# Four small half-row products behind the spreading of the token scale, in six places of a four-layer decoder trunk

## The chip, the cores and the metric

The kernel runs on one core of one Trainium2 chip. The metric is device time in microseconds (us) for one execution. Several executions are timed, and the figure for a kernel is the median of them. One more execution is recorded instruction by instruction; its own time stands beside the median below.

## The reference

The trunk has four layers on 256 tokens of width 1024. Each layer has a token mixer (layers 0 and 3: dilated window attention; layer 1: short gated convolution; layer 2: a conformer convolution module), and then a gated convolutional channel mixer with an inner width of 2816. RMS normalisation stands before and after every sub-layer:

```python
def conv_ffn(x, w_in, w_conv, w_out):
    u = causal_dwconv(x @ w_in, w_conv)
    g, v = jnp.split(u, 2, axis=-1)
    return (jax.nn.silu(g) * v) @ w_out

    for i in range(DEPTH):
        a = rms_norm(h, mix_norm_pre[i])
        ...
        h = h + rms_norm(m, mix_norm_post[i])
        f = conv_ffn(rms_norm(h, ffn_norm_pre[i]), ffn_w_in[i], ffn_w_conv[i], ffn_w_out[i])
        h = h + rms_norm(f, ffn_norm_post[i])
```

All inputs are float32, and 253.87 MB of weights are read once.

## The kernel before, in words

Features lie on the 128 partitions and the 256 tokens on the free axis, so an activation of width 1024 is eight tiles of 128x256. A weight is split into two parts for accuracy: ScalarE copies the high part (`whi`, L192) and VectorE subtracts it from the original to get the low part (`wlo`, L198). Activations are split in the same way. Each product of a weight tile (128x128, the stationary operand) with an activation tile (128x256, the moving operand) is then three TensorE instructions: high by high, high by low, low by high. `mm3` issues them at L280, L281 and L282; `Slabs.mm` issues the same three at L522. A piece of 1024 weight columns is thus 24 products.

Every mixer begins with `start_norm` (L449): a "ramp" (L433, L438, L440) over the first four pieces with the activations not yet divided by their root mean square, and in it `rstd_of` (L306), which reduces the squares over the partitions. The scale per token, r, has to lie along the free axis in all partitions; `spread` (L320 to L324) makes it so with two products of r, broadcast, with the identity (each is two passes in the trace, so four rows of L324). `spread_later` (L333) defers this: it gives back a function that calls `spread` and copies the result out of PSUM on ScalarE (L336). The channel mixer (`ffn`), `short_conv` and `conformer` hand that function to the next `column` (L462), which calls it behind the first 9 of its 24 products. Attention calls `spread` in another way and does not use `spread_later`.

A channel mixer has 22 pairs of columns; the ramp has done two pairs, and the other 20 pairs follow (L280 to L282, into PSUM banks of the pools A and B), with products of finished inner channels with the output weights between them and behind them (14 "slabs" and 8 pieces of "tail", L522). These are 62 pieces of 24 products, of which the first 9 products lie ahead of the spread. In all of them the stationary operand is a weight.

In attention two kinds of products differ. `scores` (L897) takes the product of queries and keys of two heads at a time, and a head is 64 rows: the two heads' products lie on rows 0 to 63 and rows 64 to 127 and alternate, each into a bank of its own. `value` (L878, L879, L880) has the activation as the stationary operand and the weight as the moving one. `warm` (L331) issues products of no use while TensorE would wait.

The kernel is written in program order; a framework adds the semaphores. Each engine runs its instructions in that order.

Of the kernel before, what the change touches and what calls it, by code (L numbers as in the profile page):

```python
# [10 lines left out]
F32 = mybir.dt.float32  # L11
# [5 lines left out]
P = 128  # L17
# [7 lines left out]
DH = 64  # L25
# [203 lines left out]
def trunk_kernel(ctx: ExitStack, tc: tile.TileContext, xT, pos, params, consts, masks, w8, out):  # L229
    nc = tc.nc  # L230
# [30 lines left out]
    def act(dt=F32, tag="act", bufs=NACT, shape=(P, 2, T)):  # L261
        counter[0] += 1
        return ap.tile(list(shape), dt, tag=tag, name=f"{tag}{counter[0]}", bufs=bufs)

    def two():
        t = act(F32R)
        return t[:, 0, :], t[:, 1, :]
# [7 lines left out]
    def psum(tag="A"):  # L275
        counter[0] += 1
        return ps.tile([P, 512], F32, tag=tag, name=f"ps{tag}{counter[0]}", bufs={"A": 4, "B": 3, "S": 1}[tag])
# [6 lines left out]
    def TT(out, a, b, op):  # L284
        nc.vector.tensor_tensor(out=out, in0=a, in1=b, op=op)  # L285
# [14 lines left out]
    def rstd_of(accs):  # L300


        ms = psum("S")
        for i, acc in enumerate(accs):
            for c in range(2):
                nc.tensor.matmul(ms[:, c:c + 1], lhsT=acc[:, c * P:(c + 1) * P], rhs=ones[:, 0:1],  # L306
                                 start=i == 0 and c == 0, stop=i == len(accs) - 1, skip_group_check=True)
        v, y, u, r = tiny(), tiny(), tiny(), tiny()
        nc.vector.reciprocal(out=v, in_=ms[:, 0:2])
        nc.scalar.activation(out=y, in_=ms[:, 0:2], func=AF.Sqrt)  # L310
        TT(u, y, y, ALU.mult)
        TT(r, y, v, ALU.mult)
        STT(u, u, -0.5, v, ALU.mult, ALU.mult)
        STT(r, u, 1.5, r, ALU.add, ALU.mult)
        return r
# [4 lines left out]
    def spread(r):  # L320

        rb = psum("S")[:, :T]
        for c in range(2):
            nc.tensor.matmul(rb[:, c * P:(c + 1) * P], lhsT=r[:, c:c + 1].to_broadcast([P, P]), rhs=ident,  # L324
                             start=True, stop=True)
        return rb
# [3 lines left out]
        for _ in range(n):  # L330
            nc.tensor.matmul(o, lhsT=ident, rhs=cst[:, :T], start=True, stop=True)  # L331

    def spread_later(r):  # L333

        rb = act()[:, 0, :]
        return rb, lambda: nc.scalar.copy(out=rb, in_=spread(r))  # L336

    def bc2(a):
        return a.rearrange("p (s t) -> p s t", s=1).to_broadcast([P, 2, T])
# [85 lines left out]
    def ramp(xs, os, hook=None):  # L425


        ws = [st.take() for _ in os]
        alone = [i == 0 or os[i - 1].tensor is not o.tensor for i, o in enumerate(os)]

        def second(k):
            for o, (whi, wlo, _) in zip(os, ws):
                nc.tensor.matmul(o, lhsT=whi[:, k, :], rhs=xs[k][1], start=False, stop=k == KD - 1,  # L433
                                 skip_group_check=True)

        for k in range(KD):
            for o, (whi, wlo, _), a in zip(os, ws, alone):
                nc.tensor.matmul(o, lhsT=whi[:, k, :], rhs=xs[k][0], start=k == 0 and a, stop=False,  # L438
                                 skip_group_check=True)
                nc.tensor.matmul(o, lhsT=wlo[:, k, :], rhs=xs[k][0], start=False, stop=False,  # L440
                                 skip_group_check=True)
            if k:
                second(k - 1)
        if hook:
            hook()
        second(KD - 1)
        return os

    def start_norm(xs, acc, os):  # L449

        r = []
        ramp(xs, os, lambda: r.append(rstd_of([acc])))
        return r[0]
# [5 lines left out]
    def halves(t):  # L459
        return [t[:, e * T:(e + 1) * T] for e in range(2)]  # L460
# [96 lines left out]
    def ffn(l, mg, rb):  # L557
        xs, acc = boundary(mg, rb, f"fpre{l}")
        gs = []

        pend = []

        def gate(last=False):

            ts = pend.pop(0)
            TT(ts[1], ts[0], ts[1], ALU.mult)
            x = two()
            nc.scalar.copy(out=x[0], in_=ts[1])
            st.diff()
            TT(x[1], ts[1], x[0].bitcast(F32), ALU.subtract)  # L570
            st.copy()
            gs.append(x)

        def evac(bank, f):
            u = act()
            TT(u, bank[:].rearrange("p (s t) -> p s t", s=2), bc2(rb), ALU.mult)
            ts = taps3([u[:, e, :] for e in range(2)], f"fconv{l}_", (f, KF + f), between)
            nc.scalar.activation(out=ts[0], in_=ts[0], func=AF.Silu)
            pend.append(ts)
            if len(pend) > 1:  # L580
                gate()
            if f == KF - 1:
                gate()

        banks = [psum("A") for _ in range(4)] + [psum("B") for _ in range(3)]
        rb, scale = spread_later(start_norm(xs, acc, halves(banks[0]) + halves(banks[1])))
        nc.scalar.preload_act_table(AF.Silu)
        slabs, out_ = Slabs(), None
        for what, i in ffn_steps():
            if what == "col":  # L590
                if i > 1:
                    bank = banks[i] if i < 7 else psum("B")
                    for o in halves(bank):
                        column(xs, o, scale)
                        if scale:
                            for f in range(2):
                                evac(banks[f], f)
                        scale = None
                    evac(bank, i)
                    between()  # L600
            elif what == "slab":
                slabs.add(gs[i])
                between()
            else:
                if out_ is None:
                    out_ = Out(f"fpost{l}")
                o = slabs.tail(i, gs[FF_HEAD:])
                out_.evac(i, o)
                if out_.n < KD - 1:
                    st.pump(2)  # L610
        return out_.end()


    def short_conv(l, mg, rb):
        xs, acc = boundary(mg, rb, f"mpre{l}")
        banks = [psum(a) for a in "AAAABB"]
        os = halves(banks[0]) + [banks[1][:, :T], banks[2][:, :T]]
        rb, scale = spread_later(start_norm(xs, acc, os))
        rb2 = act()[:, 0, :]
        os.append(column(xs, banks[2][:, T:], scale))  # L620
        nc.scalar.activation(out=rb2, in_=rb, func=AF.Square)
        os.append(column(xs, banks[3][:, :T]))
        ys = []
        slabs, out_ = Slabs(), None
        for what, k in sc_steps():
            if what == "col":
                if k > 1:
                    o1, o2 = banks[4:6] if k == 2 else (psum("B"), psum("B"))
                    os = halves(o1) + [o2[:, :T]]
                    for o in os:  # L630
                        column(xs, o)
                c, hh, b = os[:3]
                os = os[3:]
                t, y = tmp(), tmp()
                nc.scalar.copy(out=t, in_=c)
                TT(t, hh, t, ALU.mult)
                TT(t, t, rb2, ALU.mult)
                u, = taps3([t], "sconv", [k], between)
                TT(y, b, rb, ALU.mult)
                TT(y, y, u, ALU.mult)  # L640
                x = two()
                nc.scalar.copy(out=x[0], in_=y)
                between()
                TT(x[1], y, x[0].bitcast(F32), ALU.subtract)
                between()
                ys.append(x)
            elif what == "slab":
                slabs.add(ys[k])
                between()
            else:  # L650
                if out_ is None:
                    out_ = Out(f"mpost{l}")
                o = slabs.tail(k, ys[SC_HEAD:])
                out_.evac(k, o)
                if out_.n < 4:
                    st.pump(1)
        return out_.end()


    def conformer(l, mg, rb):  # L660
        xs, acc = boundary(mg, rb, f"mpre{l}")
        NP = KD // 2
        banks = [[psum("A") for _ in range(2)] for _ in range(2)]
        rb, scale = spread_later(start_norm(xs, acc, halves(banks[0][0]) + halves(banks[0][1])))
        nc.scalar.preload_act_table(AF.Sigmoid)
        us, ts, os = [None] * NP, [None] * NP, [None] * NP

# [88 lines left out]
        r = rstd_of([s[:, e, :] for s in sq[2:] for e in range(2)] + [sq[0][:, 0, :]])  # L756
        warm(3)
        rb = spread(r)
# [3 lines left out]
        for q in range(NP):  # L762
            if q:
                TT(us[q], us[q], bc2(rb), ALU.mult)
            for e in range(2):
# [4 lines left out]
                x, y = two(), tmp()  # L770
# [13 lines left out]
        for d in range(4, KD):  # L784
            o = column(ys, psum("B")[:, :T])
# [310 lines left out]
    with tc.manual_schedule():  # L1096
# [15 lines left out]
        mg, rb = None, None  # L1112
        for l in range(DEPTH):
            mg, rb = (attention, short_conv, conformer)[l % 3](l, mg, rb)
# [3 lines left out]
            mg, rb = ffn(l, mg, rb)  # L1118
# [83 lines left out]
```

## Time and profile before

| what | value |
|---|---|
| median of 3 runs | 1577.72 us |
| the three runs | 1564.25, 1577.72, 1581.02 us |
| profiled execution, its own time | 1583.57 us |
| profiled execution, span | 1581.7 us |
| mean granted TensorE clock | 0.996 |
| TensorE busy | 98% of the span |
| VectorE, ScalarE busy | 79%, 58% |

The span runs from the first to the last instruction of the profiled execution. Matmuls overlap each other in TensorE, so their durations do not add up to time; what a stretch of them costs is read from the distance between the starts of successive ones. The granted clock is given as a share of full speed.

### The profile page before, as it was taken

The numbers are of one execution on the slowest core, as the hardware profiler recorded it, in microseconds if no ns is written. First come the engines' busy times: TensorE is split into PE (matmuls) and PEld (weight loads), VectorE is DVE, ScalarE is ACT, GpSimd is POOL, SyncE is SP. The second block draws the span as 40 slices with busy tenths as digits, with TensorE's granted clock in tenths as the row PEclk, the third lists the DMA queues.
The fourth block names the chain that finished last, engine by engine and source line by source line (L and its number), as shares of the span: only waits on it lengthen the run. The fifth ranks groups of instructions, "written<-read, shape, count | busy, mean of one in ns | idle before, by whom it ended". The sixth has DMA issues, their size and how long they took to land.

```text
span 1581.7 us, 31426 instructions
## 1 busy us (share of the span) xinstructions
PE 1555.7 (98%) x13146; PEld 1520.5 (96%) x13146; DVE 1243.0 (79%) x2177; ACT 925.2 (58%) x1623; POOL 17.9 (1%) x51
## 2 busy tenths in 40 slices
PE   6999999999999999999999999999999999999998
PEld 6999999999999999999999999999999999999997
DVE  4997877697876779889599598786887778588783
ACT  6564655575564566656477666565655445566562
POOL 4000000000000000000000000000000000000000
PEclk9999999999999999999999999999999999999999
DMA  5653543265552644655243136554453434236540
GB/s 218 216 212 131 176 145 108 99 232 204 187 190 100 217 161 162 238 187 184 110 144 124 54 118 239 197 174 153 178 192 138 161 134 160 107 134 237 190 160 28
DMA packets 36718, 256.94 MB, mean 162 GB/s; under 512 B 4320, under 2 KB 4448, under 8 KB 5984
## 3 DMA queue, kind: packets, MB, share of 16 engines
q1 hardware_dynamic: 36288, 254.93, 45.0%
q8 instruction: 103, 1.69, 0.4%
q14 instruction: 39, 0.32, 0.1%
q10 hardware_dynamic: 288, 0.01, 0.0%
HBM read 253.87 MB, written 1.05 MB: 161 GB/s over the span
## 4 chain that ended last, share of the span: by engine, by line
PE 93%; DVE 3%; ACT 1%; POOL 1%; issue 1%; DMA 1%; DVEq 0%; ACTq 0%; POOLq 0%
PE psA L522 17%; PE psB L282 10%; PE psB L280 10%; PE psB L281 10%; PE psA L280 7%; PE psA L281 7%; PE psA L282 7%; PE psA L878 3%; PE psA L880 3%; PE psA L879 3%; PE psB L715 2%; PE psB L926 2%; PE psB L897 2%; PE psA L438 2%; PE psB L915 2%; PE psA L433 2%
## 5 line engine op out<-in xcount | busy, mean ns | idle before, releaser
L198 DVE TENSOR_TENSOR wlo<-raw,whi 128x1024 fp32r<-128x1024 f32 x480 | 580.7, 1221 | 35.3 <-ACT whi L192 34.4
L192 ACT CAST whi<-raw 128x1024 fp32r<-128x1024 f32 x480 | 490.9, 1048 | 23.8 <-DMA raw<-in_w_dram 18.7
L282 PE MATMUL psB<-act,wlo 128*128 128x256 f32 x1392 | 390.7, 281 | 0.0
L280 PE MATMUL psB<-act,whi 128*128 128x256 f32 x1392 | 390.7, 281 | 0.0
L281 PE MATMUL psB<-act,whi 128*128 128x256 f32 x1392 | 390.7, 281 | 0.0
L280 PE MATMUL psA<-act,whi 128*128 128x256 f32 x1040 | 299.2, 288 | 8.0 <-ACT whi L192 7.1
L282 PE MATMUL psA<-act,wlo 128*128 128x256 f32 x1040 | 290.7, 280 | 0.5 <-DVE wlo L198 0.5
L281 PE MATMUL psA<-act,whi 128*128 128x256 f32 x1040 | 290.8, 280 | 0.2
L522 PE MATMUL psA<-act,whi 128*128 128x256 f32 x1536 | 272.9, 281 | 0.0
L281 PEld LDWEIGHTS psB<-act,whi 128*128 128x128 f32 x1392 | 265.0, 190 | 0.0
L282 PEld LDWEIGHTS psB<-act,wlo 128*128 128x128 f32 x1392 | 263.1, 189 | 0.0
L280 PEld LDWEIGHTS psB<-act,whi 128*128 128x128 f32 x1392 | 261.3, 188 | 0.0
L522 PEld LDWEIGHTS psA<-act,whi 128*128 128x128 f32 x1536 | 236.2, 189 | 0.0
L522 PE MATMUL psA<-act,wlo 128*128 128x256 f32 x768 | 215.8, 281 | 0.0
L280 PEld LDWEIGHTS psA<-act,whi 128*128 128x128 f32 x1040 | 196.9, 189 | 12.8 <-ACT whi L192 7.1
L282 PEld LDWEIGHTS psA<-act,wlo 128*128 128x128 f32 x1040 | 197.1, 190 | 0.8 <-DVE wlo L198 0.8
L281 PEld LDWEIGHTS psA<-act,whi 128*128 128x128 f32 x1040 | 197.2, 190 | 0.6 <-DVE act L285 0.5
L291 ACT ACTIVATE tmp<-act,par 128x256 f32<-128x256 f32 x176 | 80.2, 503 | 167.5 <-DVE act L285 167.5
L288 DVE SCALAR_TENSOR_TENSOR tmp<-act,par,tmp 128x255 f32<-128x255 f32 (+1 forms) x352 | 146.7, 480 | 19.7 <-ACT tmp L291 19.7
L522 PEld LDWEIGHTS psA<-act,wlo 128*128 128x128 f32 x768 | 145.2, 189 | 0.0
L285 DVE TENSOR_TENSOR act<-psB,act 128x512 f32<-128x512 f32 (+2 forms) x94 | 58.5, 626 | 89.1 <-PE psB L282 52.2
L878 PE MATMUL psA<-whi,act 128*128 128x256 f32 x384 | 111.0, 289 | 0.0
(124 smaller groups left out, 2116.1 us busy)
## 6 DMA issues: line engine op xcount, KB each, us to landing
raw<-in_w_dram SPq DMA_DIRECT2D x239, 1024.0 KB, 4.8
h<-in_xT_dram SPq DMA_DIRECT2D x4, 256.0 KB, 5.0
raw<-in_w_dram SPq DMA_DIRECT2D x2, 512.0 KB, 5.5
out_dram<-h SPq DMA_DIRECT2D x4, 256.0 KB, 2.0
msk<-in_masks_dram SPq DMA_DIRECT2D x1, 512.0 KB, 9.3
par<-in_params_dram SPq DMA_DIRECT2D x1, 484.0 KB, 10.0
cst<-in_consts_dram SPq DMA_DIRECT2D x1, 132.0 KB, 5.9
par<-in_params_dram ACTq DMA_DIRECT2D x1, 4.0 KB, 2.9
```

Of the source, the lines that this page charges most:

```text
L192: self.nc.scalar.copy(out=hi, in_=raw)
L198: self.nc.vector.tensor_tensor(out=lo, in0=raw, in1=hi.bitcast(F32), op=ALU.subtract)
L280: nc.tensor.matmul(o, lhsT=whi, rhs=x[0], start=first, stop=False)
L281: nc.tensor.matmul(o, lhsT=whi, rhs=x[1], start=False, stop=False)
L282: nc.tensor.matmul(o, lhsT=wlo, rhs=x[0], start=False, stop=last)
L285: nc.vector.tensor_tensor(out=out, in0=a, in1=b, op=op)
L288: nc.vector.scalar_tensor_tensor(out=out, in0=a, scalar=s, in1=b, op0=op0, op1=op1)
L291: nc.scalar.activation(out=out, in_=a, func=AF.Identity, scale=s, bias=b)
L522: nc.tensor.matmul(o, lhsT=a, rhs=b, start=first and i == 0, stop=last and i == 2, skip_group_check=True)
L878: nc.tensor.matmul(oc, lhsT=xh, rhs=whi[:, k % 4, :], start=k == 0, stop=False)
L879: nc.tensor.matmul(oc, lhsT=xh, rhs=wlo[:, k % 4, :], start=False, stop=False)
L880: nc.tensor.matmul(oc, lhsT=xl, rhs=whi[:, k % 4, :], start=False, stop=k == KD - 1)
```

## The change

`spread_later` gets two more arguments, a tile pair `x` (the first activation tile, high and low part) and two PSUM banks of pool B. Behind the spread and the ScalarE copy it issues `settle`: twice, one product on rows 0 to 63 into the first bank and one on rows 64 to 127 into the second, each with 128 columns of x's high part as the stationary and 128 columns of its low part as the moving operand, as plain float32. Nothing reads the results; the banks are overwritten by the products that use them next. In the channel mixer and the short convolution the banks are ones that the code already holds; in the conformer two are taken from pool B for it. The two functions are called in six places of the program: four channel mixers, the short convolution, the conformer.

```diff
+    def settle(x, os):
+
+
+        for _ in range(2):
+            for half, o in enumerate(os):
+                rows = slice(half * DH, (half + 1) * DH)
+                nc.tensor.matmul(o, lhsT=x[0].bitcast(F32)[rows, 0:P], rhs=x[1].bitcast(F32)[rows, 0:P], start=True,
+                                 stop=True, skip_group_check=True)
+
-    def spread_later(r):
+    def spread_later(r, x, banks):
 
         rb = act()[:, 0, :]
-        return rb, lambda: nc.scalar.copy(out=rb, in_=spread(r))
+
+        def fill():
+            o = spread(r)
+            nc.scalar.copy(out=rb, in_=o)
+            settle(x, [b[:, 0:P] for b in banks])
+
+        return rb, fill
...
-        rb, scale = spread_later(start_norm(xs, acc, halves(banks[0]) + halves(banks[1])))
+        rb, scale = spread_later(start_norm(xs, acc, halves(banks[0]) + halves(banks[1])), xs[0], banks[5:7])
...
-        rb, scale = spread_later(start_norm(xs, acc, os))
+        rb, scale = spread_later(start_norm(xs, acc, os), xs[0], banks[4:6])
...
-        rb, scale = spread_later(start_norm(xs, acc, halves(banks[0][0]) + halves(banks[0][1])))
+        rb, scale = spread_later(start_norm(xs, acc, halves(banks[0][0]) + halves(banks[0][1])), xs[0],
+                                 [psum("B") for _ in range(2)])
```

The order on TensorE at the spread of the first channel mixer, before: the last products of the first nine, the spread (L324, into the bank psS), and the next products of the same column. The names are those of the tiles, with running numbers; what an instruction waits for stands in brackets.

```order
L280 MATMUL psA_3784<-act_3747,whi 128x256
L281 MATMUL psA_3784<-act_3747,whi 128x256
L282 MATMUL psA_3784<-act_3747,wlo 128x256
L324 MATMUL psS_3909<-cst,tiny_3887 128x128 [waits DVE_49,Activation_49]
L324 MATMUL psS_3909<-cst,tiny_3887 128x128
L280 MATMUL psA_3784<-act_3749,whi 128x256
L281 MATMUL psA_3784<-act_3749,whi 128x256
L282 MATMUL psA_3784<-act_3749,wlo 128x256
```

The same place with the change (L339 is the product in `settle`; each is two passes on the engine, as those of L324 are):

```order
L282 MATMUL psA_3784<-act_3747,wlo 128x256
L324 MATMUL psS_3909<-cst,tiny_3887 128x128 [waits DVE_49,Activation_49]
L324 MATMUL psS_3909<-cst,tiny_3887 128x128
L339 MATMUL psB_3787<-act_3738 128x128
L339 MATMUL psB_3788<-act_3738 128x128
L339 MATMUL psB_3787<-act_3738 128x128
L339 MATMUL psB_3788<-act_3738 128x128
L280 MATMUL psA_3784<-act_3749,whi 128x256
L281 MATMUL psA_3784<-act_3749,whi 128x256
```

Four products have come in between the spread and the rest of the column, with no wait of their own; nothing else moved. The orders of VectorE, ScalarE, GpSimd and SyncE are the same as before.

## Rows read from the trace of the kernel before

**Rows 1.** The page: span, busy time of each engine, the granted TensorE clock in 40 equal slices, and the chain of work that ended last, by engine.

```profile
span 1581.7 us, 31426 instructions
PE 1555.7 (98%) x13146; PEld 1520.5 (96%) x13146; DVE 1243.0 (79%) x2177; ACT 925.2 (58%) x1623; POOL 17.9 (1%) x51
...
PEclk9999999999999999999999999999999999999999
...
PE 93%; DVE 3%; ACT 1%; POOL 1%; issue 1%; DMA 1%; DVEq 0%; ACTq 0%; POOLq 0%
```

**Rows 2.** Windows: busy time of each engine (and instructions that touch the window) in the stretch from each of the six spreads to the end of the products that follow it without interruption. In order: channel mixer of layer 0, short convolution, channel mixers of layers 1, 2 and 3, conformer. Behind the engines stand granted clock, DMA share, GB/s.

```profile
core 0: us, PE busy (x) PEld busy (x) DVE busy (x) ACT busy (x) POOL busy (x), PEclk, DMA share, GB/s
...
310.77:484.85 174.08, 174.08 (x1481) 174.08 (x1480) 142.57 (x226) 107.57 (x170) 0.00 (x0) 1.00 0.56 200
502.80:580.77 77.97, 77.97 (x665) 77.97 (x663) 60.69 (x93) 46.25 (x72) 0.00 (x0) 1.00 0.60 216
599.00:773.06 174.06, 174.06 (x1480) 174.06 (x1479) 143.68 (x227) 108.70 (x171) 0.99 (x8) 1.00 0.56 200
923.14:1097.21 174.07, 174.07 (x1480) 174.07 (x1479) 143.58 (x227) 108.51 (x171) 0.00 (x0) 1.00 0.56 200
1396.23:1570.31 174.08, 174.08 (x1480) 174.08 (x1479) 134.62 (x219) 100.07 (x162) 0.00 (x0) 1.00 0.46 164
790.98:801.14 10.16, 10.16 (x88) 10.16 (x87) 9.33 (x22) 8.85 (x19) 0.00 (x0) 1.00 0.31 106
```

**Rows 3.** Timeline of TensorE: a product of the last two columns of attention in layer 0, the one 93 products later, and the last product of the channel mixer of layer 0 (start, duration, line, tile).

```profile
281.63 0.28 PE L280 MATMUL psB<-act,whi 128*128 128x256 f32 x1
...
292.17 0.28 PE L280 MATMUL psB<-act,whi 128*128 128x256 f32 x1
...
484.73 0.28 PE L522 MATMUL psA<-act,wlo 128*128 128x256 f32 x1
```

**Rows 4.** Timeline of TensorE around the spread (L324) in the channel mixer of layer 0.

```profile
309.98 0.28 PE L281 MATMUL psA<-act,whi 128*128 128x256 f32 x1
310.09 0.28 PE L282 MATMUL psA<-act,wlo 128*128 128x256 f32 x1
310.21 0.60 PE L324 MATMUL psS<-cst,tiny 128*128 128x128 f32 x4
310.57 0.36 PE L280 MATMUL psA<-act,whi 128*128 128x256 f32 x1
310.77 0.28 PE L281 MATMUL psA<-act,whi 128*128 128x256 f32 x1
```

**Rows 5.** Timeline of TensorE around half-row products (L897, 64 rows) in attention of layer 0, with a column behind them.

```profile
65.57 0.28 PE L280 MATMUL psA<-act,whi 128*128 128x256 f32 x1
65.69 0.28 PE L281 MATMUL psA<-act,whi 128*128 128x256 f32 x1
65.81 0.28 PE L282 MATMUL psA<-act,wlo 128*128 128x256 f32 x1
66.01 0.39 PE L897 MATMUL psB<-act 64*128 64x256 f32 x2
66.24 0.40 PE L897 MATMUL psB<-act,act 64*128 64x256 f32 x4
66.47 0.61 PE L897 MATMUL psB<-act 64*128 64x128 f32 x8
67.01 0.39 PE L280 MATMUL psA<-act,whi 128*128 128x256 f32 x1
67.23 0.28 PE L281 MATMUL psA<-act,whi 128*128 128x256 f32 x1
```

**Rows 6.** One line's instructions in a stretch (duration in ns, least, median and most; first and last start): columns behind half-row products, the first, an exception and the last of 25 such places; and a value block (L880) behind half-row products, one of 8.

```profile
L282 PE MATMUL psA<-act,wlo x15: 276/276/276, 67.7 to 72.5; 128*128 128x256 f32 x15
...
L282 PE MATMUL psA<-act,wlo x8: 281/281/282, 210.8 to 213.3; 128*128 128x256 f32 x8
...
L282 PE MATMUL psA<-act,wlo x3: 276/276/276, 1354.3 to 1355.0; 128*128 128x256 f32 x3
...
L880 PE MATMUL psA<-whi,act x8: 279/279/282, 102.8 to 105.3; 128*128 128x256 f32 x8
```

**Rows 7.** The same view for the slabs of the channel mixer of layer 0 and of the short convolution (L522), for the ramp of two stages (L438), and for columns into pool B at the end of the conformer (L282).

```profile
L522 PE MATMUL psA<-act,whi x352: 281/281/281, 337.9 to 484.6; 128*128 128x256 f32 x176
...
L522 PE MATMUL psA<-act,whi x128: 281/281/281, 541.2 to 580.5; 128*128 128x256 f32 x128
...
L438 PE MATMUL psA<-act,whi x29: 281/281/313, 298.1 to 307.6; 128*128 128x256 f32 x29
...
L438 PE MATMUL psA<-act,whi x22: 276/276/281, 492.5 to 499.6; 128*128 128x256 f32 x22
...
L282 PE MATMUL psB<-act,wlo x32: 276/276/277, 894.4 to 904.9; 128*128 128x256 f32 x32
```

**Rows 8.** Windows: the first 35 us of the channel mixer of layer 1; and the timeline of VectorE and of TensorE there, where the low part of a weight piece is made (L198) and first used (L282).

```profile
599.00:634.00 35.00, 35.00 (x300) 35.00 (x299) 34.53 (x57) 24.76 (x40) 0.00 (x0) 1.00 0.54 189
...
606.43 1.23 DVE L198 TENSOR_TENSOR wlo<-raw,whi 128x1024 fp32r<-128x1024 f32 x1
...
609.35 0.28 PE L282 MATMUL psB<-act,wlo 128*128 128x256 f32 x1
```

**Rows 9.** One line's instructions in a stretch (duration in ns, least, median and most; first and last start): the ramp in the second half of the conformer and the ramp of attention in layer 3, each behind a place where TensorE had waited.

```profile
L438 PE MATMUL psA<-act,whi x29: 276/276/277, 884.0 to 893.0; 128*128 128x256 f32 x29
...
L438 PE MATMUL psA<-act,whi x24: 281/281/384, 1105.0 to 1112.9; 128*128 128x256 f32 x24
```

**Rows 10.** The longest waits of TensorE in the span and the one for a low part of weights: line that waited, what for, us in total, times, longest.

```profile
PE psA L280 <- ACT whi L192: 7.1, 1, 7.1
...
PE psB L897 <- DVE act L285: 1.7, 2, 0.8
PE psS L324 <- DVE tiny L288: 1.2, 7, 0.2
PE psA L280 <- ACT act L422: 0.9, 2, 0.5
...
PE psA L282 <- DVE wlo L198: 0.5, 1, 0.5
```

## The prediction

> **What bounds the kernel now.** I read the page first: TensorE is busy for 98% of the span and carries 93% of the chain that ended last [rows 1]. So whatever TensorE does not do faster gains nothing, and anything put on it is paid in full unless it shortens something else. Next I read the windows from each of the six spreads to the end of the uninterrupted products behind it [rows 2]. TensorE is busy throughout there, at a granted clock of 1.00, and nothing else is full over the whole stretch (VectorE 142.57 of 174.08 us). In these stretches time is the number of products times the distance from one start to the next.
>
> That distance is the third reading, and it has two values for one and the same instruction. In the channel mixer of layer 0 the start moves from 310.77 [rows 4] to 484.73 [rows 3]. The mixer has 62 x 24 = 1488 products behind the ramp, 310.77 is the 11th, so these are 1477 steps: 173.96 / 1477 = 117.8 ns. In the last columns of attention 31 high-part products (93 steps of three-term products) take 292.17 - 281.63 = 10.54 us [rows 3]: 113.3 ns. Lines, shapes and types agree, and so does the clock (full speed, the 2.4 GHz level). The profile's duration of a product, whose end is modelled, is a handy mark: 276 ns goes with 113.3 (call it the fast step), 281 ns with 117.8 (the slow one). The difference is 4.45 ns, 3.8%.
>
> It is a state of the engine and not of the code: the same ramp runs slow in one channel mixer (281) and fast in the short convolution (276) [rows 7]. In all six stretches of [rows 2] it is slow. The rows around the spread show it being set: the starts ahead of L324 are 0.11 apart, those behind it 0.12 in the long run [rows 4], and by the windows it stays so up to the next reduction.
>
> **What half-row products do to it.** In attention, half-row products (L897) come right before a column in 25 places. In [rows 5] the steps before are slow (65.57, 65.69, 65.81); behind the block the first two gaps are long, and from the seventh step on the column runs fast: 276 for all low-part products from 67.7 to 72.5 [rows 6]. So it is at 24 of the 25 places, whichever step came before; the exception, at 210.8 (281), stands behind a block that had been interrupted by a wait (one of the two of L897, 0.8 us at the longest [rows 10]). Before a value block, where the stationary operand is an activation, the result is the slow step, 8 times of 8 (279 to 282, the row of L880). `settle` ends like `scores`: plain float32, 64 rows against 128 columns, halves in turn, two banks. What follows it is L280 with a weight as the stationary operand, so the 25 places are the nearest rows, not the 8.
>
> **The change part by part.** *Removed:* nothing. *Moved:* nothing; the other engines' orders are as before. The ScalarE copy of the scale still hangs on L324 alone, so VectorE's backlog there starts no later.
>
> *Added:* four products, eight passes, at six places. Price of one, from [rows 5]: entering costs 0.20 (65.81 to 66.01); the first pair of passes to the second 0.23 (66.01 to 66.24); four pairs of 128 columns and the way out take 0.54 (66.47 to 67.01), of which the way out is about 0.20 as the way in, so a pair takes 0.11, both halves side by side; the first full-row product to the second 0.22 (67.01 to 67.23). Together 0.20 + 0.22 + 0.11 + 0.11 + 0.20 + 0.22 = 1.06. This takes the place of what stands behind L324 now: 0.36 for four passes and the step to L280, three of them 0.11, leaves 0.03, and then 0.20 to L281 [rows 4], 0.23. So 0.83 us each, **+5.0 us** for six. Bounds: if switching costs nothing, four pairs at 0.11, 0.45 each and 2.7 in all; if the halves run one behind the other, 8 x 0.11 + 0.62 - 0.23, 1.27 each and 7.6 in all. I take the middle value because it comes from the same form of instruction.
>
> *Changed step:* if the fast step holds from each settle to the end of its stretch, the weight loads counted in [rows 2] gain 4.45 ns each: 1480 + 663 + 1479 + 1479 + 1479 + 87 = 6667, less some four slow ones at each start: **-29.7 us**. The channel mixers carry 26.3 of it, the short convolution 3.0, the conformer 0.4 (there plain float32 products of another kind come after 87).
>
> Does it hold? Columns into pool B hold it (32 low-part products, 276 to 277), and so does a ramp that changes bank and weight with each pair (22 at 276, one reading of 281) [rows 7]. The slabs (L522) were never seen in it: 281 in all 352 and 128 readings. They issue the same three terms with weights stationary, so I expect them to hold it too.
>
> Does a faster TensorE begin to wait? The tightest place is the opening of the channel mixers in layers 1 and 2, where VectorE is busy for 34.53 of 35.00 us [rows 8]. Counting pieces in order, the low part of the fifth column's weights is ready at 606.43 + 1.23 = 607.66 and first used at 609.35: 1.69 us to spare. By then four pieces of 24 have gained 0.43 us, and settle has put TensorE 0.83 us back. So nothing waits there, and later the supply runs further ahead, since VectorE has a sixth of each mixer idle [rows 2].
>
> *Sum* on the profiled execution: 1583.57 - 29.7 + 5.0 = 1558.9. The four slow steps at each start and the ramps, whose state also shifts (92 products at 4.45 ns is 0.4 us each, either way), are worth a microsecond; I say **1558.5 us**. The median of the runs shown, 1577.72, is 5.85 below the profiled execution and the lowest run 19 below. One channel mixer in the fast step would explain 6.6 us, so those runs may have had a stretch or two fast by chance; that is an estimate, the trace holds one execution. If the change fixes the step, this does not come on top.
>
> **The rivals.**
> 1. *Nothing gained, settle paid* (ends on the other side). The step stays slow behind settle, because what stands ahead of it is L324 and not a column, or because it is not the half rows that set it. Then 1583.57 + 5.0 = 1588.6 (1586.3 to 1591.2). For it: the value blocks come out slow 8 times of 8, and L324 leaves the slow step at all six spreads. Against it: 24 of 25 columns. It decides from 0.83 us / 4.45 ns = 187 fast products per settle: fewer, and the change costs time. [...]
> 2. *Reached and lost on the way.* If the first slab ends the fast step, a channel mixer gains only up to 337.9 [rows 7], (337.9 - 310.77) / 117.8 ns = 230 products, 1.0 us; the short convolution up to 541.2, 1.4 us; conformer 0.4. 4 x 1.0 + 1.4 + 0.4 - 5.0 is +0.8 us the good way: 1582.8. If instead a wait of TensorE redraws the step, it can come out either way, as the ramps behind two waits do (276 and 281 [rows 9]). Half of the 26.3 us of the mixers lost would give 1558.9 + 13 = 1572. For it: no row of a fast L522. Against it: of TensorE's waits, those for weights (7.1 and 0.5 us) and the others listed are few [rows 10], and TensorE is busy without a gap in all six stretches [rows 2].
> 3. *Fast everywhere, but dearer switching* (7.6): 1561.5. This stays within the forecast's own range.
>
> **How the numbers follow.** Fast in all or nearly all of the stretches: 0.72, at 1558.5, own range 1552 to 1566 (bounds of settle's price, ramps, and a few us from the attention layers, whose columns show both steps and can fall otherwise in another execution). Rival 2: 0.14, between 1566 and 1583. Rival 1: 0.14. A measurement of this kernel can tell about 1% from no change; 1% below the median is 1561.9, 1% above is 1593.5. The forecast lies below 1561.9 in some five cases of six, 0.60, and a little comes from partial cases whose attention fell well: faster 0.61. Rivals 1 and 2 lie within 1%, with the rest of the forecast: same 0.36. Slower 0.03, if rival 1 comes with more than its dear bound. The range 1551 to 1578 holds the forecast and most of rival 2, about 0.82.
>
> **What would show it.** Right: eight passes of L339 at each spread, in pairs some 3 to 10 ns apart; about 1.06 us from the last L324 pass to the second full-row product; then starts 0.113 apart and durations of 276 in L280 to L282 and in L522 up to the next L306; windows of some 167.5 us where there were 174.1. Wrong: 281 behind L339 (rival 1), 276 in columns and 281 from the first L522 (rival 2), or idle time on TensorE before `wlo` in the opening of layers 1 and 2.

## The result, and the profile after

| | before | changed |
|---|---|---|
| median of 20 runs | 1580.88 us | 1566.61 us |
| lowest, highest | 1564.25, 1584.70 us | 1558.56, 1568.64 us |
| profiled execution, own time | 1583.57 us | 1566.16 us |
| ratio to before, 95% interval | | 0.9915 [0.9897, 0.9932] |

By the ratio the change makes the kernel 0.85% faster, and the interval does not reach 1. Of the 20 runs, 17 lie between 1565.98 and 1568.64 us and three lower, at 1558.56, 1560.10 and 1561.92.

The windows of the changed kernel over the same six stretches as in [rows 2], from the second full-row product behind settle to the next reduction, in order of layers; the last row is the conformer. The columns are those of [rows 2].

```profile
core 0: us, PE busy (x) PEld busy (x) DVE busy (x) ACT busy (x) POOL busy (x), PEclk, DMA share, GB/s
311.55:479.06 167.51, 167.51 (x1479) 167.51 (x1479) 142.26 (x226) 107.53 (x169) 0.00 (x0) 1.00 0.58 208
497.83:572.88 75.05, 75.05 (x664) 75.05 (x663) 60.72 (x93) 45.51 (x71) 0.00 (x0) 1.00 0.60 218
591.91:759.43 167.52, 167.52 (x1479) 167.52 (x1479) 143.32 (x227) 108.39 (x170) 0.94 (x8) 1.00 0.57 208
911.32:1078.84 167.52, 167.52 (x1480) 167.52 (x1480) 143.29 (x227) 108.35 (x170) 0.00 (x0) 1.00 0.58 208
1378.84:1552.91 174.07, 174.07 (x1479) 174.07 (x1479) 134.32 (x219) 99.74 (x161) 0.00 (x0) 1.00 0.45 164
778.46:788.22 9.76, 9.76 (x87) 9.76 (x87) 9.31 (x22) 8.95 (x20) 0.00 (x0) 1.00 0.33 110
```

Five stretches run at the fast step: the mixers of layers 0 to 2 take 167.5 us where they took 174.1, the short convolution 75.0 for 78.0. The mixer of layer 3 takes 174.07, as before. The granted clock is 1.00 in all of them, and TensorE has no gap in any. The slabs (L522 before, L537 now) show the same two states, here in layer 0 and in layer 3 (duration in ns, least, median, most):

```profile
L537 PE MATMUL psA<-act,whi x352: 276/276/276, 337.6 to 478.8; 128*128 128x256 f32 x176
...
L537 PE MATMUL psA<-act,whi x352: 281/281/281, 1405.9 to 1552.7; 128*128 128x256 f32 x176
```

The timeline of TensorE around settle (L339), in layer 0 and in layer 3:

```profile
309.92 0.28 PE L281 MATMUL psA<-act,whi 128*128 128x256 f32 x1
310.03 0.28 PE L282 MATMUL psA<-act,wlo 128*128 128x256 f32 x1
310.14 0.60 PE L324 MATMUL psS<-cst,tiny 128*128 128x128 f32 x4
310.68 0.72 PE L339 MATMUL psB<-act 64*128 64x128 f32 x8
311.32 0.39 PE L280 MATMUL psA<-act,whi 128*128 128x256 f32 x1
311.55 0.28 PE L281 MATMUL psA<-act,whi 128*128 128x256 f32 x1
...
1377.06 0.28 PE L281 MATMUL psA<-act,whi 128*128 128x256 f32 x1
1377.17 0.28 PE L282 MATMUL psA<-act,wlo 128*128 128x256 f32 x1
1377.35 0.68 PE L324 MATMUL psS<-cst,tiny 128*128 128x128 f32 x4
1377.96 0.71 PE L339 MATMUL psB<-act 64*128 64x128 f32 x8
1378.61 0.39 PE L280 MATMUL psA<-act,whi 128*128 128x256 f32 x1
1378.84 0.28 PE L281 MATMUL psA<-act,whi 128*128 128x256 f32 x1
```

In layer 0 the spread starts 0.11 us behind the product before it. In layer 3 it starts 0.18 behind it: TensorE waited there for the scale r, and only there of the six places. From the spread to the second full-row product is 1.41 us in layer 0 (310.14 to 311.55), against 0.56 before (310.21 to 310.77 [rows 4]): settle costs 0.85 us.

The wait comes from the chain that makes r (reciprocal on VectorE, L309, then the square root on ScalarE, L310). The timeline of both engines, in layer 0 and in layer 3:

```profile
308.76 0.17 DVE L309 RECIPROCAL tiny<-psS 128x2 f32<-128x2 f32 x1 [1.47 <-PE psS L306]
...
309.02 0.17 ACT L310 ACTIVATE tiny<-psS 128x2 f32<-128x2 f32 x1 [3.86 <-DVE tiny L309]
...
1375.90 0.17 DVE L309 RECIPROCAL tiny<-psS 128x2 f32<-128x2 f32 x1 [1.48 <-PE psS L306]
...
1376.45 0.17 ACT L310 ACTIVATE tiny<-psS 128x2 f32<-128x2 f32 x1 [4.15 <-DVE tiny L309]
```

The square root starts 0.26 us behind the reciprocal in layer 0 and 0.55 behind it in layer 3. ScalarE had been idle; what held it the other 0.29 us the trace does not show. It is not a chance of one execution: in layer 3 the square root starts 0.54 to 0.55 us behind the reciprocal in four of the traced kernels (the changed one and, by their labels in the table below, e1_full_rows, e4_after12 and e6_lower_only), and about 0.26 us behind it in the eight others.

### The profile page after: what moved, and what is told of

Read it like the earlier page. It is cut to its first block, busy times and chain, and to the rows that moved or that the text cites. A ratio compares the mean times of both kernels' runs of the same rounds, so it can differ in the third digit from the quotient of the medians.

```text
span 1564.3 us, 31521 instructions
## 1 busy us (share of the span) xinstructions
PE 1538.2 (98%) x13194; PEld 1501.4 (96%) x13194; DVE 1243.2 (79%) x2177; ACT 925.8 (59%) x1623; POOL 17.9 (1%) x51
## 4 chain that ended last, share of the span: by engine, by line
PE 93%; DVE 3%; ACT 1%; POOL 1%; issue 1%; DMA 1%; DVEq 0%; ACTq 0%; POOLq 0%
PE psA L537 17%; PE psB L280 10%; PE psB L282 10%; PE psB L281 10%; PE psA L280 7%; PE psA L281 7%; PE psA L282 7%; PE psA L894 3%; PE psA L895 3%; PE psA L896 3%; PE psB L731 2%; PE psB L942 2%; PE psB L913 2%; PE psA L453 2%; PE psB L931 2%; PE psA L448 2%
## 5 line engine op out<-in xcount | busy, mean ns | idle before, releaser
L198 DVE TENSOR_TENSOR wlo<-raw,whi 128x1024 fp32r<-128x1024 f32 x480 | 580.2, 1220 | 34.6 <-ACT whi L192 33.9
L282 PE MATMUL psB<-act,wlo 128*128 128x256 f32 x1392 | 385.6, 277 | 0.0
L280 PE MATMUL psB<-act,whi 128*128 128x256 f32 x1392 | 385.6, 277 | 0.0
L281 PE MATMUL psB<-act,whi 128*128 128x256 f32 x1392 | 385.6, 277 | 0.0
L280 PE MATMUL psA<-act,whi 128*128 128x256 f32 x1040 | 298.6, 287 | 8.0 <-ACT whi L192 7.1
L282 PE MATMUL psA<-act,wlo 128*128 128x256 f32 x1040 | 290.0, 279 | 0.5 <-DVE wlo L198 0.5
L281 PE MATMUL psA<-act,whi 128*128 128x256 f32 x1040 | 290.1, 279 | 0.2
L537 PE MATMUL psA<-act,whi 128*128 128x256 f32 x1536 | 265.1, 277 | 0.0
L282 PEld LDWEIGHTS psB<-act,wlo 128*128 128x128 f32 x1392 | 262.5, 189 | 0.0
L537 PEld LDWEIGHTS psA<-act,whi 128*128 128x128 f32 x1536 | 231.7, 188 | 0.0
L537 PE MATMUL psA<-act,wlo 128*128 128x256 f32 x768 | 212.9, 277 | 0.0
L282 PEld LDWEIGHTS psA<-act,wlo 128*128 128x128 f32 x1040 | 196.9, 189 | 0.8 <-DVE wlo L198 0.8
L537 PEld LDWEIGHTS psA<-act,wlo 128*128 128x128 f32 x768 | 144.9, 189 | 0.0
L922 ACT ACTIVATE act<-act,tiny 128x512 f32<-128x512 f32 x64 | 46.4, 725 | 110.3 <-DVE tiny L920 110.3
```

The source lines that it names most:

```text
L198: self.nc.vector.tensor_tensor(out=lo, in0=raw, in1=hi.bitcast(F32), op=ALU.subtract)
L280: nc.tensor.matmul(o, lhsT=whi, rhs=x[0], start=first, stop=False)
L281: nc.tensor.matmul(o, lhsT=whi, rhs=x[1], start=False, stop=False)
L282: nc.tensor.matmul(o, lhsT=wlo, rhs=x[0], start=False, stop=last)
L537: nc.tensor.matmul(o, lhsT=a, rhs=b, start=first and i == 0, stop=last and i == 2, skip_group_check=True)
```

## The experiments

Two questions were put: is it the half rows that set the fast step, and why did layer 3 stay slow. The table sums up all profiled executions; the text behind it takes the runs one by one. "f" is a stretch at the fast step from settle (or the spread) to its end, "s" at the slow one, and "w" marks that TensorE waited for r ahead of the spread. The times are medians where more than one run was made. M0 to M3 are the channel mixers, SC the short convolution, CF the conformer.

| kernel | M0 | SC | M1 | CF | M2 | M3 | time, us (runs) |
|---|---|---|---|---|---|---|---|
| before | s | s | s | s | s | s | 1580.88 (20) |
| changed | f | f | f | f | f | s w | 1566.61 (20) |
| e1_full_rows | s | s | s | s | s | f w | 1584.94 (1) |
| e2_once | f | f | f | f | f | f | 1557.79 (1) |
| e3_ahead | f | f | s | f | f | f | 1566.01 (1) |
| e4_after12 | f | f | f | f | f | f | 1560.96 (4) |
| e5_after6 | f w | f w | f w | s w | f w | f w | 1559.79 (1) |
| e6_lower_only | f | f | f | f | f | f w | 1563.10 (1) |
| e7_none_after6 | f w | s w | f w | f w | s w | s w | 1573.10 (1) |
| e8_once_after12 | f | f | f | f | f | f | 1558.79 (5) |
| e9_none_after12 | s | s | s | s | s | s | 1582.82 (10) |
| e10_after6_timed | f w | f w | f w | s w | s w | f w | 1567.36 (4) |

### Full rows in place of half rows

```diff
-                rows = slice(half * DH, (half + 1) * DH)
+                rows = slice(0, P)
```

> The four products of settle stand where they stood but on all 128 rows; everything else is as in the changed kernel. Theory H (going to 64 rows and back sets the step): the engine never changes its row mode, so all six stretches behind the spread run at the slow step, 174.1 us for a channel mixer, durations 281; eight passes at 0.11 us cost 0.9 us at each of six places; time about 1583.6 + 5.3 = 1589, between 1586 and 1591. Rival R (any four products, or any 0.9 us of delay there, shift the step): five of six stretches fast as in the changed kernel, 167.5 us for a mixer, time about 1566.

Measured: 1584.94 us. The five places where TensorE did not wait are slow, as theory H said; rival R falls. The sixth, layer 3, is fast, which neither theory had said and which puts the time below the 1586 to 1591 us of theory H. Windows of the mixers of layers 0 and 3, and the timeline of TensorE at the spread of layer 3:

```profile
312.10:486.08 173.98, 173.98 (x1480) 173.98 (x1479) 142.24 (x226) 107.25 (x169) 0.00 (x0) 1.00 0.55 200
1404.18:1571.60 167.42, 167.42 (x1480) 167.42 (x1479) 134.31 (x219) 99.97 (x161) 0.00 (x0) 1.00 0.48 170
```

```profile
1402.35 0.28 PE L281 MATMUL psA<-act,whi 128*128 128x256 f32 x1
1402.46 0.28 PE L282 MATMUL psA<-act,wlo 128*128 128x256 f32 x1
1402.64 0.68 PE L324 MATMUL psS<-cst,tiny 128*128 128x128 f32 x4
1403.16 1.06 PE L339 MATMUL psB<-act 128*128 128x128 f32 x8
1403.97 0.37 PE L280 MATMUL psA<-act,whi 128*128 128x256 f32 x1
```

The spread again starts 0.18 us behind the last product: the place that waited. In the changed kernel the place that waited was the slow one of six, here it is the fast one. A wait ahead of the spread thus went with the other step in both kernels, and the runs further down test it.

### One pair in place of two

```diff
-        for _ in range(2):
+        for _ in range(1):
```

> settle issues one pair of half-row products and not two. Theory H: one switch to half rows and back is enough; the same stretches fast (167.5 us for a channel mixer in layers 0 to 2), and each place about 0.22 us cheaper, 1.3 us in all: about 1565 if layer 3 is slow as in the changed kernel's profile, about 1558 if it is fast. Rival: the number of products behind the spread is what shifts the step (a phase that each product moves on); then with half of them some or all stretches come out slow, 6.6 us for each channel mixer, up to 1585.

Measured: 1557.79 us, all six places fast. One pair of half-row products is enough, and the count of products is not what does it. No place waited in this execution; r was done 300 ns ahead of the spread's first weight load in layer 3.

### Settle ahead of the spread

```diff
         def fill():
+            settle(x, [b[:, 0:P] for b in banks])
             o = spread(r)
             nc.scalar.copy(out=rb, in_=o)
-            settle(x, [b[:, 0:P] for b in banks])
```

> settle stands ahead of the spread and not behind it; the same products. Theory H, with the spread itself (L324) as what sets the slow step last: all six stretches slow, 174.1 us for a channel mixer, about 1583.6 + 5.0 = 1588.6. Rival: the half rows set the step wherever they stand and the spread keeps it: five or six stretches fast, 1559 to 1566.

Measured: 1566.01 us, five places fast. Here theory H failed in its second half: with half-row products just ahead of it, the spread left the fast step at five of six places. Without them it left the slow step at all 12 places where nothing waited (the kernel before, and the control e9_none_after12 below). The rival's count came true, but its reason, that the half rows set the step and the spread keeps it, does not hold at the sixth place, layer 1. Windows of the mixers of layers 0 and 1:

```profile
310.80:478.20 167.40, 167.40 (x1480) 167.40 (x1479) 142.62 (x226) 107.84 (x170) 0.00 (x0) 1.00 0.58 208
591.50:765.46 173.96, 173.96 (x1479) 173.96 (x1478) 143.58 (x227) 108.50 (x171) 1.00 (x8) 1.00 0.55 200
```

Layer 1 differs in what comes first. Timeline of TensorE in layer 0 (fast behind the spread) and in layer 1 (slow), and the durations of one line in the columns ahead of settle, in the same order:

```profile
309.03 0.28 PE L280 MATMUL psA<-act,whi 128*128 128x256 f32 x1
309.15 0.28 PE L281 MATMUL psA<-act,whi 128*128 128x256 f32 x1
309.26 0.28 PE L282 MATMUL psA<-act,wlo 128*128 128x256 f32 x1
309.47 0.71 PE L339 MATMUL psB<-act 64*128 64x128 f32 x8
310.12 0.71 PE L324 MATMUL psS<-cst,tiny 128*128 128x128 f32 x4
...
589.76 0.28 PE L280 MATMUL psA<-act,whi 128*128 128x256 f32 x1
589.87 0.28 PE L281 MATMUL psA<-act,whi 128*128 128x256 f32 x1
589.98 0.28 PE L282 MATMUL psA<-act,wlo 128*128 128x256 f32 x1
590.19 0.71 PE L339 MATMUL psB<-act 64*128 64x128 f32 x8
590.84 0.71 PE L324 MATMUL psS<-cst,tiny 128*128 128x128 f32 x4
...
L282 PE MATMUL psA<-act,wlo x3: 279/281/281, 308.6 to 309.3; 128*128 128x256 f32 x3
...
L282 PE MATMUL psA<-act,wlo x3: 276/276/276, 589.3 to 590.0; 128*128 128x256 f32 x3
```

Ahead of settle the columns run at the slow step in layer 0 and at the fast one in layer 1. At all five places that came out fast the columns ahead were slow, and at the sixth they were fast. In this execution half rows followed by the spread thus turned the step round at every place rather than setting it. With a single fast stream among the six, that this is a rule is not shown.

### The spread behind 12 products, so that nothing waits

```diff
-    def column(xs, o, hook=None):
+    def column(xs, o, hook=None, at=3):
...
-            if hook and k == 3:
+            if hook and k == at:
...
-                        column(xs, o, scale)
+                        column(xs, o, scale, 4)
```

(and the same `4` in the short convolution and the conformer)

> The spread, the copy and settle stand behind 12 products of their column and not behind 9, so that TensorE comes to the spread 0.34 us later. About layer 3, whose mixer was slow in the changed kernel's profile. Theory W: it was slow because TensorE had to wait for the scale r there (r done 116 ns ahead of the spread's first weight load, against 251 to 358 at the five places that came out fast), and the wait moved the phase in which settle began. Then no place waits now, all four channel mixers take 167.5 us, and the median falls by 6.6 us to about 1559.5 (1557 to 1562). Theory P: it is where layer 3's tiles and banks lie; layer 3 stays slow at 174.1 us and the median at about 1566.5.

Measured: 1560.96 us, four runs from 1560.04 to 1561.47, ratio 0.9866 [0.9823, 0.9910]. In the traced run all six places are fast, layer 3 too, where r was now done 317 ns ahead. One line's durations in the columns of that mixer:

```profile
L282 PE MATMUL psB<-act,wlo x288: 276/276/276, 1390.3 to 1515.1; 128*128 128x256 f32 x144
```

The square root of layer 3 was as late as in the changed kernel (0.54 us behind the reciprocal); only the wait of TensorE was gone. Theory P falls: layer 3's tiles and banks are the same as in the changed kernel.

### The spread behind 6 products, so that everything waits

The same edit with `2` in place of `4`.

> The changed kernel with the spread and settle behind 6 products of the column and not 9, so that TensorE comes 0.34 us sooner to the spread, before the scale r is done (it was done 251 to 358 ns ahead at five places): nearly all six places wait for r by up to 0.1 us. Theory W (a wait ahead of the spread shifts the phase in which settle begins, and settle then leaves the slow step): the places that wait come out slow, up to all six, 174.1 us for each channel mixer, about 1589 us at most. Theory W2 (a wait only draws the phase anew): a mixture of fast and slow places, each slow mixer 6.6 us, 1565 to 1585. Theory P (layer 3's tiles and banks): only layer 3 slow, about 1566.

Measured: 1559.79 us. All six places waited, and five came out fast; the slow one was the conformer's short stretch. Theory W, by which the places that wait come out slow, falls; P falls once more. W2 is left, though the time lies below the span it gave. The same kernel once more, with four runs:

> The changed kernel with the spread and settle behind 6 products, where all six places waited for r, once more and timed. Theory W2 (a wait draws the phase anew): the executions differ, most places fast and now and then a mixer slow: times between 1558 and 1573, in steps of some 6.6 us. If the one look (1559.79) stands for all executions, they lie within 2 us of it, and a wait ahead of the spread is not what makes layer 3 slow in the changed kernel.

Measured: 1567.36 us (1566.84 to 1568.71), ratio 0.9913 [0.9892, 0.9934], 7.6 us above the single run. All six waited again; now the mixer of layer 2 is slow, and the conformer. Timeline of TensorE in layer 2:

```profile
910.27 0.28 PE L281 MATMUL psA<-act,whi 128*128 128x256 f32 x1
910.39 0.28 PE L282 MATMUL psA<-act,wlo 128*128 128x256 f32 x1
910.53 0.68 PE L324 MATMUL psS<-cst,tiny 128*128 128x128 f32 x4
911.14 0.71 PE L339 MATMUL psB<-act 64*128 64x128 f32 x8
911.79 0.39 PE L280 MATMUL psA<-act,whi 128*128 128x256 f32 x1
```

The spread starts 0.14 us behind the last product, a wait of some 0.02, and the step behind settle is slow. So the same code comes out either way once a wait stands ahead of it, as W2 says. The four runs agree with each other, though, so that it is not drawn anew in each execution, and neither of the two expectations came true as it was written. The single run was made on another chip than the four (the record has chip 2 and chip 3); whether that is the difference no run shows.

### Only the lower half

```diff
-                rows = slice(half * DH, (half + 1) * DH)
+                rows = slice(0, DH)
```

> All four products of settle on rows 0 to 63, into the two banks in turn. They can't run side by side now, so that settle takes 0.11 us for each of eight passes, 0.43 us more at each place, 2.6 us in all. Theory H (the switch to 64 rows and back sets the step): stretches as fast as in the changed kernel, 1562 if all six are fast, 1568.6 with one mixer slow. Rival (the two halves side by side do it): all six slow, about 1591.

Measured: 1563.10 us, all six places fast, layer 3 too, though it waited. The two halves side by side are not needed. It costs what was expected of eight passes one behind the other, so two halves in turn are the cheaper form.

### The wait alone, without settle

The kernel before, with the spread behind 6 products.

> The kernel before, without settle, with the spread behind 6 products and not 9, so that TensorE waits for r ahead of the spread at nearly all six places. In the run with full-row products the one place where the spread had waited came out fast, the five others slow. Theory W (the wait itself can set the step, half rows or not): some or all stretches fast without any added product; all fast would be 1583.6 - 29.7 + 0.6 = about 1554.5, three of four mixers fast about 1561. Theory H alone (only a change of row mode sets it): all slow, about 1584.

Measured: 1573.10 us. All six places waited; the mixers of layers 0 and 1 and the conformer are fast, the other three slow. One line's durations in the columns of the mixers of layer 0 and layer 3:

```profile
L282 PE MATMUL psB<-act,wlo x288: 276/276/276, 321.6 to 446.4; 128*128 128x256 f32 x144
...
L282 PE MATMUL psB<-act,wlo x288: 281/281/281, 1396.1 to 1525.8; 128*128 128x256 f32 x144
```

Half rows are thus not the only thing that can give the fast step; a wait of TensorE ahead of the spread can too, but not dependably. The place behind 6 products was not run without a wait. Against the place as the cause speaks the run with full rows, where the one place that waited stood behind 9 products and came out fast.

### The later place alone, and with one pair

The kernel before, with the spread behind 12 products, as a control for e4_after12:

> Control for the place: the kernel before, without settle, with the spread behind 12 products and not 9, so that no place waits for r. If the half rows set the step and not the later place, all six stretches run slow, 174 us for each channel mixer, and the time is that of the kernel before (about 1583). If the later place alone did it in the runs that had both, up to all six are fast, and the time is about 1554.

Measured: 1582.82 us, ratio 1.0009 [0.9994, 1.0023], all six places slow. One line's durations in the columns of the mixer of layer 3:

```profile
L282 PE MATMUL psB<-act,wlo x288: 281/281/281, 1407.3 to 1537.0; 128*128 128x256 f32 x144
```

The later place does nothing by itself. With settle of one pair:

> One pair of half-row products, and the spread behind 12 products, so that no place waits for r. By theories H and W all six stretches fast in every execution: 1.3 us less than the run with the spread behind 12 products and two pairs (1560.96), about 1559.5, all runs within 2 us of each other. Rival (one pair is too little and came out well by chance): one or two mixers slow in some executions, 1566 to 1573.

Measured: 1558.79 us, five runs from 1558.22 to 1559.61, ratio 0.9853 [0.9833, 0.9873]. All six places are fast, and the runs lie within 1.4 us. The ratio is below that of the changed kernel (0.9915 [0.9897, 0.9932]). That it is faster than one pair behind 9 products (1557.79 us, one run) is not shown.

### What the runs say together

Where half-row products stand behind the spread, and TensorE did not wait ahead of it, all 28 places came out fast (5 in the changed kernel, 6 with one pair, 6 and 6 with the spread behind 12 products, 5 with the lower half). Where it waited, 10 of 14 did. Without half rows and without a wait none of 17 did (6 before, 5 with full rows, 6 in the control), and with a wait 4 of 7. Each kernel was traced once, so these are counts of places and not of repeated executions.

## Why the prediction came out as it did

The range (1551 to 1578) holds the median of 1566.61, and the direction was right. The point, 1558.5, was 8.1 us too low, and the gain of 0.85% is within the 1% that was called no change; the larger chance had been given to more. That the range held the result is in part luck: the forecast's own range was 1552 to 1566, and 1566.61 lies in the part (1566 to 1583) that had been added for rival 2, which did not happen.

- *Two steps at one clock, set at a switch.* Right: 113.3 against 117.8 ns again, at a granted clock of 1.00, and full rows in the same place leave the slow step.
- *The price of settle.* Right: 0.85 us measured in layer 0, 0.83 forecast.
- *The fast step holds to the end.* Right, and L522 was the doubt: L537 shows 276 in all 352 readings of layer 0. TensorE has no gap in any stretch, so the faster engine met no late weights, and nothing was lost on the way as rival 2 had it.
- *"If the fast step holds from each settle to the end of its stretch ... -29.7 us."* This term was mis-sized. The five fast stretches give 3 x 6.54 + 2.90 + 0.34 = 22.9 us by the starts of their first and last products (174.16 to 167.62 for a mixer, 78.05 to 75.15, 10.21 to 9.87). The mixer of layer 3 gave nothing, 6.6 us of the 29.7. The rest of the sum fits: 22.9 - 6 x 0.85 = 17.8, and the span fell by 1581.7 - 1564.3 = 17.4.
- *Why layer 3.* The prediction took 24 of 25 columns as the rate, and named the exception, a block with a wait in it, without following it up: a wait next to the half-row products. Counted again in the trace before, half-row blocks stand right before a column 24 times and not 25, and 23 of the columns are fast. All 22 behind blocks without a wait are fast. The two other blocks each hold a wait of 0.83 us: the column behind the one at 208.41 is slow [rows 6], the one behind the block at 1294.07 is fast:

```profile
1295.74 0.49 PE L897 MATMUL psB<-act 64*128 64x128 f32 x4 [0.83 <-DVE act L285]
...
L282 PE MATMUL psA<-act,wlo x8: 276/276/279, 1296.5 to 1298.9; 128*128 128x256 f32 x8
```

  So a wait already went with either outcome there. The prediction looked for waits inside the stretches (rival 2, "a wait of TensorE redraws the step") and not ahead of the spread, where r was only 253 to 363 ns early in the trace before. The runs show that the wait matters: without one 28 of 28 places are fast, and 10 of 14 with one. That this one wait made layer 3 slow in the changed kernel is borne out by the run with the spread behind 12 products: it removed the wait, its trace shows layer 3 fast, and its four times leave no room for a slow mixer. A wait does not make layer 3 slow every time: with the lower half alone it waited and was fast.
- *The three low runs* of the changed kernel (1558.56 to 1561.92) are at the time of the kernels with all six places fast. No trace of them exists, so that layer 3 was fast in them is argued, not shown. The same holds for the spread of the kernel before (1564.25 to 1584.70).
- *Rival 1* (nothing gained) did not happen. One of its grounds was read rightly: L324 leaves the slow step where no half rows stand with it and nothing waits; half rows behind it undo that. The other, value blocks that come out slow 8 times of 8, was misread: their 279 ns says nothing of the step of a column. In the trace before, four of these eight value blocks have a column right behind them, with no half rows between, and it is fast. One line of one such block, and one of the column behind it:

```profile
L880 PE MATMUL psA<-whi,act x8: 278/279/279, 152.9 to 155.3; 128*128 128x256 f32 x8
...
L282 PE MATMUL psA<-act,wlo x8: 276/276/277, 155.7 to 158.1; 128*128 128x256 f32 x8
```

Open is what it is in TensorE that half rows set and a wait shifts (the expectations call it a phase), why the same kernel came out differently in the single run and in the four later ones, and what held ScalarE for 0.29 us ahead of its square root in layer 3.

## What to carry to other kernels

Where TensorE bounds a kernel, read the distance between starts of equal products in several stretches before taking one value as the engine's pace: 3.8% lay between two stretches of the same code here. A cheap change of row mode (0.22 us a pair and 0.62 for going in and out, by [rows 5]) in front of a long stretch can be worth it, with two pairs as here from some 190 products on, but put it where TensorE does not wait just ahead. A count of outcomes in the trace before, such as the prediction's 24 of 25, is worth reading for what its exception had beside it, and for the other places that had the same beside them.

## What the runs showed of the hardware

- A stream of 128x256 products with the weight stationary ran at 113.3 or 117.8 ns from start to start, at a granted clock of 1.00 (the 2.4 GHz level) in both, and kept its step to the end of a channel mixer (1479 products), through changes of weights, banks and lines.
- Half-row products ahead of a weight-stationary column gave the fast step (28 of 28 places without a wait); with the four full-row passes of the spread between them and the column, five slow streams turned fast and one fast stream turned slow (one execution).
- A wait of 0.02 to 0.12 us ahead of the spread is enough to change which step the next 174 us run at: 4 of 7 places fast with it and none of 17 without, no half rows in either.
